# A hybrid decoder layer in fp32: pairs of tiles loaded as one, new homes for half of x, small transfers moved to GpSimd

## The chip, the cores and the metric

The kernel runs on one NeuronCore of a Trainium2 chip. The metric is the device time of one execution in microseconds (us); lower is better. The engines are PE (TensorE, matrix products, with its weight loads as PEld), DVE (VectorE), ACT (ScalarE), POOL (GpSimd) and SP (SyncE, which here only issues DMAs). Each takes its instructions strictly in the order in which they stand on its own queue. Data move between DRAM and the on-chip SBUF by DMAs, which two queues issue: SP's and GpSimd's.

## The reference

The layer takes x of 1024 tokens × 2048 channels and a memory of 256 tokens, all fp32:

```python
h = rmsnorm(x, ln_g)
proj = h @ w_in            # columns: g_u g_v g_z | d_q d_k d_v d_z d_a d_b | c_q c_z
out_a = gmlp_spatial_gating(g_u, g_v, gmlp_ws, gmlp_bs, gmlp_ln_g, gmlp_ln_b) * silu(g_z)
q, k, v = causal_conv_silu(concat(d_q, d_k, d_v), conv_w)      # 4 taps; q and k l2-normalised
g = -exp(dn_a_log) * softplus(d_a + dn_dt_bias); beta = sigmoid(d_b)
out_b = rmsnorm(gated_delta_rule(q, k, v, g, beta), dn_norm_g) * silu(d_z)   # 8 heads of 128
mk, mv = split(rmsnorm(mem, mem_norm_g) @ w_mem_kv)            # 4 heads of 128
out_c = softmax(c_q mk^T / sqrt(128)) mv * silu(c_z)
x = x + concat(out_a, out_b, out_c) @ w_out
return rmsnorm(x, final_g)
```

## The kernel before

**Precision.** An fp32 operand is split into a high part (`ahi`, `whi`: a cast to fp32r, which ACT does) and the rest (`alo`, `wlo`: a subtraction, on DVE), and each product is three matmuls: high·high, high·low, low·high.

**The big products.** The contraction over 2048 channels is cut into KT = 16 tiles of P = 128. The 1024 tokens are two halves of HT = 512. A product over a pair of column blocks is seen as a product of 2 × 2 block matrices (token half by contraction half, and contraction half by column block) and done with seven block products instead of eight, named m and run in the order 2, 1, 6, 5, 3, 7, 4. Their operands are blocks or sums and differences of blocks. `first_product` does it for the first six column tiles of the DeltaNet's q, k and v, straight from the prepared x in SBUF; `seven` does it for the five pairs of column blocks that follow (blocks 0 to 4), and for W_out. In `seven` the left operands come from DRAM for two contraction tiles at a time, by `h_left` (x's transposed blocks `h0_d`, `hT_d` and their sums `s_all`) or `m_left` (the gated mix and its sums `s_d`); the weights come in by `rights_made`, `rights_back` and, in the first product, `first_block` and `fetch`, and are combined by `meet`, `minus` and `add` on DVE. A block of weights of two contraction tiles is two DMAs of 256 KB, in the first product two or three for one tile.

**The stages.** To about 62 us the memory's K and V are made in 16 steps (`kvmark[k]` marks the end of step k), while `prep` makes the x rows 0 to 3 (a row is 128 tokens × 2048 channels in four tiles of 512): ACT squares the row and sums it up, POOL takes 1/rms (the 128x1 operations on `small`), DVE scales, PE transposes, and the result is split (`put0`). `kv_d` (kvd in the profile) takes the K and V, scaled, back to DRAM. To about 110 us comes `first_product(2)`, and beside it the second half of x, rows 4 to 7, is loaded, scaled and transposed (`prep1`; here ACT copies the transposed tile out of PE's banks `dn`), its sums are made (`left_sums`), and the per-token decays (`decay_rows`, `decay_mm`, `decays`). `first_product(1)` and the other five follow; from about 200 us the fronts (convolution, l2 norms, the q·k products in `qk`) run beside them, then blocks 0 to 4 with the DeltaNet's backs and the attention, W_out to about 1601 us, and the last normalisation.

**Buffers.** The small tiles have rings: `kT`, `qT`, `vs`, `kd` and `ai` of four tiles of 512 each, `ut`, `gt` and `inv` of two of 1024. Before the fronts need them they hold the rows of x: row 4 the halves of `ut`; row 5 two tiles of `kT` and two of `qT`; row 6 two of `kd` and two of `ai`; row 7 two of `vs` and the halves of a `gt`. Later the same tiles hold weight blocks (`kept`) and left operands (`araw`).

**The order.** The code records every operation in `Plan` before any is issued, which is why all instructions of the profile have line L300. `issue` then simulates the engines with a table of costs and gives every instruction its place: of what is ready on an engine, the one with the lowest `rank` first. `R.slow` and `R.land` are nanoseconds that it adds between another engine's result, or a landed load, and the PE instruction that uses it. They cost no time by themselves; a PE instruction with them takes a later place in PE's queue. `behind(op)` and `R.gate` keep an operation behind another.

Of the kernel before, what the change touches and what calls it, by code (L numbers as in the profile page):

```python
# [9 lines left out]
F32 = mybir.dt.float32  # L10
# [293 lines left out]
def kernel(  # L304
# [95 lines left out]
    et = [C([P, HT], f"et{i}") for i in range(2)]  # L400
    ring = {t: Slots(t, 4, [P, HT]) for t in ("kT", "qT", "vs", "kd", "ai")}
# [15 lines left out]
    h0_d = DT([KT, P, HT], "h0d")  # L417
    hT_d = DT([NH, P, HT], "hTd")
# [42 lines left out]

    def row_tiles(tag):
        if tag in ("inv", "gt", "ut"):
            return [b[:, i * HT : (i + 1) * HT] for b in (ring[tag](), ring[tag]()) for i in range(2)]
        return [ring[tag]() for _ in range(4)]
# [82 lines left out]
    def put0(tt):  # L548
        def put(q, tp):
# [9 lines left out]
            with rank(5):  # L559
                Q.dma_start(h0_d[4 * q : 4 * q + 4, :, tt * P : (tt + 1) * P].rearrange("k p n -> p k n"), t)  # L560
# [68 lines left out]
    for mt in range(2):  # L629
        t = [ring["ai"](F32R) for _ in range(2)]  # L630
# [3 lines left out]
        for i in range(2):  # L634
            with rank(2.5):
              Q.dma_start(
                kv_d[1, :, :, i, mt * P : (mt + 1) * P].rearrange("h p e -> p h e"),
                tok(t[i]).bitcast(F32),
            )
    with rank(2):  # L640
        prep(3, put0(3), spare, (2, 3, 0, 1))
    for h in range(NX):
        t = ring["vs"](F32R).rearrange("p (s m) -> p s m", s=2)
        with rank(2.2):
            split_to(t[:, 0], t[:, 1], kfs[h], V)
        with rank(2.5):
            Q.dma_start(kv_d[0, h], t.bitcast(F32))


    R.gate = kvmark[-1]  # L650
    G.affine_select(out=utri, in_=ones, compare_op=ALU.is_ge, fill=0.0, base=0,
                    pattern=[[1, P]], channel_multiplier=-1)
    with rank(3.5):
        Q.dma_start(rows[0:96], conv_w.rearrange("k (c p) -> (k c) p", p=P))
        Q.dma_start(rows[96:100], gmlp_ln_g[0].rearrange("(c p) -> c p", p=P))
        Q.dma_start(rows[100:104], gmlp_ln_b[0].rearrange("(c p) -> c p", p=P))
        Q.dma_start(rows[104:105], dn_norm_g)
    dtb = C([P, NH], "dtb")
    Q.dma_start(dtb, dn_dt_bias[0].partition_broadcast(P))
    nal = C([P, NH], "nal")  # L660
    Q.dma_start(nal, dn_a_log[0].partition_broadcast(P))
    S.activation(nal, nal, AF.Exp)
    V.tensor_scalar(nal, nal, -1.0, None, op0=ALU.mult)

    with rank(3.5):
# [3 lines left out]
        V.tensor_scalar(cw, pt[:, 0:96], 0.5, None, op0=ALU.mult)  # L669
        col2 = C([P, 9], "col2")  # L670
        V.tensor_copy(col2, pt[:, 96:105])

# [1239 lines left out]
```

## Time and profile before

| | |
|---|---|
| three runs | 1617.7, 1619.48, 1614.85 us; median 1617.7 |
| the profiled execution | 1613.38 us, its span 1611.4 us |
| granted TensorE clock, mean of the span | 0.996 of full speed |
| instructions | 26264 |
| DMA | 428.97 MB, mean 266 GB/s |
| HBM | read 337.49 MB, written 89.16 MB |

The span is the time from the first to the last instruction of the profiled execution. An engine's busy share is an average over stages, so the stretches are read one by one. In the rows of the trace, `out<-in` names the tile written and the tile read, "128x512" is partitions × elements, and the square bracket gives the time for which the engine stood idle before the instruction, and what released it.

### The profile page before, as it was taken

Reading aid. Unit: us, or ns where it says so; the run is one execution under the profiler, and the core shown is the slowest. Engines: PE = TensorE matmul, PEld = TensorE weight load, DVE = VectorE, ACT = ScalarE, POOL = GpSimd, SP = SyncE. Lnnn points to the kernel's source line nnn. Section 1 sums busy time; section 2 is a strip of 40 time slices with the busy share of each in tenths; the row PEclk is TensorE's granted clock in tenths of the full one; section 3 lists DMA queues with packets and bytes.
Section 4 is the critical chain, followed back from the end, with each engine's and each line's share of the span. In section 5 each row is a group of like instructions: output and inputs, shape, how many; then the busy total and the mean of one; then the engine's idle time right before and its main releaser. Section 6 shows DMA issues by size and latency. Waiting matters only on the chain.

```text
span 1611.4 us, 26264 instructions
## 1 busy us (share of the span) xinstructions
PE 1581.3 (98%) x8538; PEld 1325.7 (82%) x8538; DVE 1310.2 (81%) x2209; ACT 1023.9 (64%) x2185; POOL 310.8 (19%) x499
## 2 busy tenths in 40 slices
PE   9999999999999999999999999999999999999997
PEld 8878778778888888878888888888888888888886
DVE  6987797889899899887998777767778888789775
ACT  7843476576755688966676667767556774345355
POOL 0100023242311422335433333031000000000001
PEclk9999999999999999999999999999999999999999
DMA  9998878988679878888689775888867879588646
GB/s 358 299 273 238 263 221 257 327 306 273 223 252 317 271 241 279 311 308 272 213 265 362 249 235 168 273 305 285 300 224 261 260 248 351 191 279 290 215 146 240
DMA packets 264523, 428.97 MB, mean 266 GB/s; under 512 B 32905, under 2 KB 90306, under 8 KB 264386
## 3 DMA queue, kind: packets, MB, share of 16 engines
q1 hardware_dynamic: 241762, 371.03, 69.9%
q0 software_dynamic: 22016, 55.21, 10.2%
q8 instruction: 67, 1.10, 0.3%
q10 hardware_dynamic: 608, 1.06, 0.2%
q14 instruction: 70, 0.57, 0.1%
HBM read 337.49 MB, written 89.16 MB: 265 GB/s over the span
## 4 chain that ended last, share of the span: by engine, by line
PE 78%; DMA 9%; DVE 7%; ACT 2%; issue 2%; SPq 2%; POOL 0%; DVEq 0%; POOLq 0%; ACTq 0%
PE acc L300 55%; PE dn L300 23%; SPq L300 2%; DVE wlo L300 1%; DMA wraw<-in_w_in_dram 1%; DMA vs<-in_x_dram 1%; DVE qT L300 1%; DMA y<-in_w_in_dram 1%; DMA raws<-h0d 1%; DVE alo L300 1%; DMA qT<-in_w_in_dram 1%; DVE kT L300 1%; DMA kT<-in_w_in_dram 1%; DMA gd<-y2w 0%; ACT whi L300 0%
## 5 line engine op out<-in xcount | busy, mean ns | idle before, releaser
L300 PE MATMUL acc<-ahi,whi 128*128 128x512 f32 (+1 forms) x1328 | 455.5, 393 | 1.4 <-ACT y L300 1.4
L300 PE MATMUL acc<-ahi,wlo 128*128 128x512 f32 (+1 forms) x904 | 354.3, 393 | 0.0
L300 PEld LDWEIGHTS acc<-ahi,whi 128*128 128x128 f32 x1328 | 248.5, 188 | 50.3 <-ACT y L300 1.8
L300 PEld LDWEIGHTS acc<-ahi,wlo 128*128 128x128 f32 x904 | 169.9, 188 | 32.9
L300 ACT CAST ahi<-raws 128x1024 fp32r<-128x1024 f32 x141 | 147.8, 1048 | 62.5 <-PE dn L300 28.1
L300 PE MATMUL acc<-alo,whi 128*128 128x512 f32 (+1 forms) x480 | 187.5, 391 | 0.0
L300 PE MATMUL acc<-ahi,zh 128*128 128x512 f32 x424 | 167.7, 396 | 3.2 <-DVE y L300 3.2
L300 PE MATMUL acc<-ahi,zl 128*128 128x512 f32 x424 | 167.5, 395 | 0.0
L300 PE MATMUL acc<-alo,zh 128*128 128x512 f32 x424 | 167.0, 394 | 0.0
L300 POOL TENSOR_TENSOR small<-small,mhalf 128x1 f32<-128x1 f32 x26 | 20.4, 789 | 510.1 <-DVE small L300 510.1
L300 DVE TENSOR_TENSOR wlo<-wraw,whi 128x1024 fp32r<-128x1024 f32 (+1 forms) x80 | 94.3, 1179 | 22.1 <-ACT whi L300 19.9
L300 ACT CAST whi<-wraw 128x1024 fp32r<-128x1024 f32 (+1 forms) x80 | 81.4, 1017 | 47.9 <-PE acc L300 32.9
L300 PEld LDWEIGHTS acc<-alo,whi 128*128 128x128 f32 x480 | 90.7, 189 | 17.0
L300 DVE TENSOR_TENSOR alo<-raws,ahi 128x1024 fp32r<-128x1024 f32 x71 | 86.5, 1219 | 17.4 <-ACT ahi L300 17.1
L300 DVE TENSOR_TENSOR ahi<-raws,ahi 128x1024 fp32r<-128x1024 f32 x70 | 85.3, 1219 | 18.5 <-ACT ahi L300 18.2
L300 PEld LDWEIGHTS acc<-ahi,zh 128*128 128x128 f32 x424 | 79.9, 188 | 18.6 <-DVE y L300 3.6
L300 DVE TENSOR_TENSOR alo<-y,ahi 128x1024 fp32r<-128x1024 f32 x65 | 79.7, 1226 | 17.1 <-ACT ahi L300 16.9
L300 PEld LDWEIGHTS acc<-ahi,zl 128*128 128x128 f32 x424 | 79.9, 188 | 15.4
L300 PEld LDWEIGHTS acc<-alo,zh 128*128 128x128 f32 x424 | 79.9, 188 | 15.2
L300 ACT CAST ahi<-y 128x1024 fp32r<-128x1024 f32 x65 | 68.3, 1050 | 37.9 <-PE acc L300 19.5
L300 PE MATMUL dn<-whi,ahi 128*128 128x512 f32 x232 | 77.6, 389 | 0.0
L300 PE MATMUL acc<-whi,ahi 128*128 128x512 f32 x216 | 73.2, 392 | 0.0
(535 smaller groups left out, 3807.4 us busy)
## 6 DMA issues: line engine op xcount, KB each, us to landing
wraw<-in_w_in_dram SPq DMA_DIRECT2D x160, 256.0 KB, 4.3
raws<-sa SPq DMA_DIRECT2D x122, 256.0 KB, 4.2
y<-in_w_in_dram SPq DMA_DIRECT2D x80, 256.0 KB, 4.3
wraw<-in_w_out_dram SPq DMA_DIRECT2D x64, 256.0 KB, 4.3
raws<-h0d SPq DMA_DIRECT2D x58, 256.0 KB, 5.1
y<-sa SPq DMA_DIRECT2D x54, 256.0 KB, 4.3
raws<-sd SPq DMA_DIRECT2D x42, 256.0 KB, 3.0
y<-in_w_out_dram SPq DMA_DIRECT2D x33, 256.0 KB, 4.5
```

Of the source, the lines that this page charges most:

```text
L300: o.fn(*o.args, **o.kw)
```

## The change

The rings `kT`, `qT`, `vs`, `kd` and `ai` keep two tiles of 512, and the other two become one tile of 1024 each, the `twin` (`kTw` and so on). Weight blocks and left operands kept there are now one tile: one load, one cast, one subtraction of 1024 (768 in the first product) where there were two. `h0_d`, `hT_d` and `s_all` lie in DRAM by pairs of contraction tiles, so that a left pair is one load of 512 KB; `rows_of` and `twos_of` give the writes that shape, and a right operand taken from such a tile is read with a stride (`by_row`). `blk` covers two contraction tiles, `first_block` and `fetch` make a block one or two DMAs. The rows of x have other homes: row 4 the twins of `kd` and `vs`, row 5 the halves of `ut`, row 6 the halves of a `gt` and the twin of `ai`, row 7 the twins of `kT` and `qT`. The eight kvd stores and seven small loads go to GpSimd's queue; `R.slow` is 800 around the work on x's second half and around `qk`; the decay sums of the first half are made once after row 5, in another bank, and `decays` has rank 4.1 instead of 6.

In the built programs PE has the same number of matmuls of each form. SP has 1033 DMAs instead of 1518, GpSimd 391 instead of 376; DVE's additions and subtractions are 1291 instead of 1523, ACT's casts 573 instead of 643.

The places at which the order changes follow. On ACT, at the preparation of rows 4 to 7, before (`jk` takes the squares of an x tile, `small` their sum, `dn` is a bank with a transposed tile, `wraw` and `inv` hold weights):

```order
L300 ACTIVATE jk,small_97<-ai_390 128x512
L300 COPY xr_91<-dn_111 128x128
L300 ACTIVATE jk,small_98<-vs_391 128x512
L300 COPY kT_383<-dn_112 128x512
L300 COPY kT_384<-dn_111 128x512
L300 ACTIVATE jk,small_98<-vs_392 128x512
L300 ACTIVATE nal<-nal 128x8
L300 ACTIVATE jk,small_98<-gt_393 128x512
L300 COPY qT_385<-dn_112 128x512
```

and after:

```order
L300 ACTIVATE jk,small_102<-gt_376 128x512 x2
L300 ACTIVATE jk,small_102<-aiw 128x512 x2
L300 CAST inv_373<-wraw_71 128x768
L300 ACTIVATE jk,small_103<-kTw 128x512 x2
L300 CAST whi_73<-wraw_72 128x768
L300 ACTIVATE jk,small_103<-qTw 128x512 x2
L300 CAST whi_74<-inv_375 128x768
L300 COPY kdw<-dn_116 128x512
L300 COPY kdw<-dn_117 128x512
L300 COPY vsw<-dn_116 128x512
```

Before, the squares of row 7 (vs, gt) stand between the copies of row 5 (kT, qT); after, all squares of rows 6 and 7 stand ahead of the first copy of row 4 (kdw), with three weight casts among them. On SP the two loads of vs stood behind the third weight block of the first product; all x loads now stand ahead of it.

On SP, at the loads for the meets in `first_product(1)`, before (`in_w_in` is W_in; `pd` takes finished columns of the product; kd, kT and inv take pieces of weight blocks):

```order
L300 DMA pd_2_173<-y_394 128x512
L300 DMA kd_387<-in_w_in_dram 128x256
L300 DMA pd_0_179<-y_394 128x512
L300 DMA kd_388<-in_w_in_dram 128x256
L300 DMA kT_383<-in_w_in_dram 128x384
L300 DMA kT_383<-in_w_in_dram 128x128
L300 DMA pd_1_180<-y2w 128x512
L300 DMA inv_453<-in_w_in_dram 128x128 x2
L300 DMA inv_453<-in_w_in_dram 128x512
```

and after:

```order
L300 DMA pd_0_172<-y_377 128x512
L300 DMA kTw<-in_w_in_dram 128x512
L300 DMA kTw<-in_w_in_dram 128x2x128
L300 DMA pd_1_173<-y2w 128x512
L300 DMA inv_436<-in_w_in_dram 128x512
L300 DMA inv_436<-in_w_in_dram 128x2x128
L300 DMA pd_2_174<-y2w 128x512
L300 DMA raws<-sa_327 128x1024
L300 DMA aiw<-in_w_in_dram 128x512
L300 DMA aiw<-in_w_in_dram 128x2x128
```

A block is two DMAs where it was three or four, the stores of finished columns still stand between them, and a left pair (raws) is one load.

On POOL, at the end of the memory's product, before (`small_101` to `104` are the sums of four x rows; `utri` and `xr` are constants):

```order
L300 TENSOR_TENSOR small_101<-small_101,mhalf 128x1
L300 AFFINE_SELECT utri<-ones 128x128
L300 TENSOR_TENSOR small_102<-small_102,mhalf 128x1
L300 MEMSET xr_89 128x3
L300 MEMSET xr_90 128x3
L300 TENSOR_TENSOR small_103<-small_103,mhalf 128x1
L300 TENSOR_TENSOR small_104<-small_104,mhalf 128x1
```

and after (`small_108` is the sum of row 4):

```order
L300 TENSOR_TENSOR small_107<-small_107,mhalf 128x1
L300 DMA kvd<-ai_149 128x4x128
L300 DMA kvd<-ai_150 128x4x128
L300 DMA kvd<-kd_151 128x4x128
L300 DMA kvd<-kd_152 128x4x128
L300 AFFINE_SELECT utri<-ones 128x128
L300 DMA kvd<-vs_153 128x512
L300 DMA kvd<-vs_154 128x512
L300 MEMSET xr_94 128x3
L300 DMA kvd<-et_77 128x512
L300 DMA kvd<-et_78 128x512
L300 TENSOR_TENSOR small_108<-small_108,mhalf 128x1
```

The eight stores now stand between the 1/rms of row 3 and that of row 4. The seven small loads stand earlier on the same queue, ahead of the 1/rms of row 1.

The core of the diff:

```diff
-    ring = {t: Slots(t, 4, [P, HT]) for t in ("kT", "qT", "vs", "kd", "ai")}
+    et = [C([P, HT], f"et{i}", F32R) for i in range(2)]
+    for t in et:
+        R.users[t.tensor.name] = []
+    ring = {t: Slots(t, 2, [P, HT]) for t in ("kT", "qT", "vs", "kd", "ai")}
+    twin = {t: C([P, 2 * HT], f"{t}w") for t in ring}
...
-    h0_d = DT([KT, P, HT], "h0d")
-    hT_d = DT([NH, P, HT], "hTd")
+    h0_d = DT([KT // 2, P, 2 * HT], "h0d")
+    hT_d = DT([NH // 2, P, 2 * HT], "hTd")
...
-            return [b[:, i * HT : (i + 1) * HT] for b in (ring[tag](), ring[tag]()) for i in range(2)]
-        return [ring[tag]() for _ in range(4)]
+        return [ring[tag](), ring[tag](), *halves(twin[tag])]
+
+    def rows_of(d, q, tt):
+        return d[2 * q : 2 * q + 2, :, tt * 2 * P : (tt + 1) * 2 * P].rearrange("j p n -> p j n")
+
+    def twos_of(t):
+        return t.rearrange("p (j n) -> p j n", j=2)
...
-                Q.dma_start(h0_d[4 * q : 4 * q + 4, :, tt * P : (tt + 1) * P].rearrange("k p n -> p k n"), t)
+                Q.dma_start(rows_of(h0_d, q, tt), twos_of(t.rearrange("p k c -> p (k c)")))
...
-        t = [ring["ai"](F32R) for _ in range(2)]
+        t = [ring[("ai", "kd")[mt]](F32R) for _ in range(2)]
...
         for i in range(2):
             with rank(2.5):
-              Q.dma_start(
-                kv_d[1, :, :, i, mt * P : (mt + 1) * P].rearrange("h p e -> p h e"),
-                tok(t[i]).bitcast(F32),
-            )
+                G.dma_start(
+                    kv_d[1, :, :, i, mt * P : (mt + 1) * P].rearrange("h p e -> p h e"),
+                    tok(t[i]).bitcast(F32),
+                )
...
-        t = ring["vs"](F32R).rearrange("p (s m) -> p s m", s=2)
+        t = (ring["vs"](F32R) if h < 2 else et[h - 2]).rearrange("p (s m) -> p s m", s=2)
         with rank(2.2):
             split_to(t[:, 0], t[:, 1], kfs[h], V)
         with rank(2.5):
-            Q.dma_start(kv_d[0, h], t.bitcast(F32))
-
-
+            G.dma_start(kv_d[0, h], t.bitcast(F32))
...
+    R.gate = kvmark[8]
+    with rank(2.5):
+        for at, n, src in ((0, 96, conv_w.rearrange("k (c p) -> (k c) p", p=P)),
+                           (96, 4, gmlp_ln_g[0].rearrange("(c p) -> c p", p=P)),
+                           (100, 4, gmlp_ln_b[0].rearrange("(c p) -> c p", p=P)), (104, 1, dn_norm_g)):
+            G.dma_start(rows[at : at + n], src)
+        abf = ring["E"]()[:, 0 : KT * 16].rearrange("p (k c) -> p k c", c=16)
+        G.dma_start(abf, w_in[:, C_AB : C_AB + 16].rearrange("(k p) c -> p k c", p=P))
+        dtb = C([P, NH], "dtb")
+        G.dma_start(dtb, dn_dt_bias[0].partition_broadcast(P))
+        nal = C([P, NH], "nal")
+        G.dma_start(nal, dn_a_log[0].partition_broadcast(P))
...
-    s_all = [DT([NH, P, HT], f"sa{i}") for i in range(4)]
-    s_d = [[[t[j] for t in s_all] for j in range(NH)],
-           [[DT([P, HT], f"sd1_{j}_{i}") for i in range(4)] for j in range(NH)]]
+    s_all = [DT([NH // 2, P, 2 * HT], f"sa{i}") for i in range(4)]
+    s_d = [[DT([P, HT], f"sd1_{j}_{i}") for i in range(4)] for j in range(NH)]
...
     def blk(w, k, c0):
-        return w[k * P : (k + 1) * P, c0 : c0 + HT]
-
-    def whole(k):
+        return w[k * P : (k + 2) * P, c0 : c0 + HT].rearrange("(u p) c -> p u c", u=2)
...
+            V.tensor_tensor(out=tok(t), in0=ahq[q][:, tt], in1=alq[q][:, tt], op=ALU.add)
+            Q.dma_start(rows_of(h0_d, q, tt), twos_of(t))
...
-        mm(a, wk, ahi[k], k == NH, False)
-        mm(a, wk, alo[k], False, k == NH - 1)
+        mm(a, wk, ahi[k], k == 0, False)
+        mm(a, wk, alo[k], False, k == KT - 1)
...
             hs = ring["hs"]()
+            R.slow = 800.0
             kd, ai, _ = qk(h, hf, q, k, hs, gt)
+            R.slow = 0.0
...
-        return [w_in[k, c0 : c0 + n] for c0, n in FIRST_COLS[b]]
+        qk = w_in[k, C_Q : C_Q + 2 * DW].rearrange("p (s c) -> p s c", s=2)
+        return [qk[:, :, 0 : 3 * P]] if b == 0 else [w_in[k, C_DV : C_DV + HT], qk[:, :, 3 * P : 4 * P]]
+
+    def by_row(a, u):
+        return [x_.rearrange("p (t u c) -> p u t c", u=2, c=P)[:, u] for x_ in a]
...
-        for d, x_ in pieces(dst, blk_):
-            Q.dma_start(d, x_)
+
+        if len(blk_) == 2:
+            v, qk = cuts(dst)
+            Q.dma_start(v, blk_[0])
+            Q.dma_start(twos_of(qk), blk_[1])
+        elif len(dst) == 1:
+            Q.dma_start(twos_of(dst[0]), blk_[0])
+        else:
+            a, b = dst
+            Q.dma_start(a[:, 0 : 3 * P], blk_[0][:, 0])
+            Q.dma_start(a[:, 3 * P :], blk_[0][:, 1, 0:P])
+            Q.dma_start(b, blk_[0][:, 1, P:])
...
-            return [x_[:, u * HT : (u + 1) * HT] for x_ in lefts]
+            return by_row(lefts, u)
...
-    two = [[ring[tag](slot=k) for k in (2, 3)] for tag in ("kT", "qT", "kd", "ai", "vs")]
-    tiles = [[t[:, j * HT : (j + 1) * HT] for t in ring["ut"].bufs for j in range(2)],
-             two[0] + two[1], two[2] + two[3], two[4] + halves(ring["gt"]())]
-    for tag in ("kT", "qT", "vs", "kd", "ai"):
-        ring[tag].turn = (0, 1)
+    tiles = [halves(twin["kd"]) + halves(twin["vs"]), [h for t in ring["ut"].bufs for h in halves(t)],
+             halves(ring["gt"]()) + halves(twin["ai"]), halves(twin["kT"]) + halves(twin["qT"])]
...
+    R.slow = 800.0
     with rank(4):
         for i in range(NT):
             prep1(i)
             decay_rows(strips, i)
+            if i == 1:
+                a = work()
+                for k in range(KT):
+                    decay_mm(a, k)
+                S.copy(sums0, a[0:32])
...
-    for k in (*range(NH, KT), *range(NH)):
-        decay_mm(dnr.bufs[2], k)
-    with rank(6):
+    for q in range(NQ // 2, NQ):
+        for tt in range(H0, NT):
+            whole(q, tt)
+    with rank(4.1):
         decays(1, strips, lambda: dnr.bufs[3])
-        decays(0, dnr.bufs[2], lambda: dnr.bufs[2])
+        decays(0, sums0, lambda: dnr.bufs[2])
+    R.slow = 0.0
...
-    kept, vs01 = two[:4], two[4]
-    more = halves(heir(alq[2], "y3", "alo2"))
+    kept, vs01 = [[twin[t]] for t in ("kT", "qT", "kd", "ai")], halves(twin["vs"])
...
-    araw = over([kept[3], vs01, *([t] for t in raws)])
+    araw = over([[twin["vs"]], [twin["qT"]], *([t] for t in raws)])
...
-        for i, x_ in enumerate(src):
-            t = ts[i] if len(ts) == 2 else ts[0][:, i * HT : (i + 1) * HT]
-            Q.dma_start(t, x_)
+        if len(ts) == 1 and not isinstance(src, list):
+            Q.dma_start(twos_of(ts[0]) if src.ndim == 3 else ts[0], src)
+            return ts
+        for i in range(2):
+            t = ts[i] if len(ts) == 2 else halves(ts[0])[i]
+            Q.dma_start(t, src[i] if isinstance(src, list) else src[:, i])
...
-            return loaded([s_d[0][j][SUM[m]] for j in js])
-        return loaded([hT_d[j] if m == 4 else h0_d[j + NH * (m == 2)] for j in js])
+            return loaded(s_all[SUM[m]][n])
+        return loaded(hT_d[n] if m == 4 else h0_d[n + NH // 2 * (m == 2)])
...
-                    load2(ts, [blocks(0, 1, j) for j in js])
-            r = plain([blocks(*((1, 1) if m in (7, 5) else AT[m]), j) for j in js])
-            parts = [(t, r[:, i * HT : (i + 1) * HT]) for i, t in enumerate(ts)]
+                    load2(ts, blocks(0, 1, js))
+            r = plain(blocks(*((1, 1) if m in (7, 5) else AT[m]), js))
+            parts = [(ts[0], r)]
```

132 lines of the change are left out of this document (52 added, 80 removed).

## The prediction

> **What bounds the kernel.** I read the page first, then the stretches, what PE waits for, and the chain of waits.
>
> ```profile
> PE 1581.3 (98%) x8538; PEld 1325.7 (82%) x8538; DVE 1310.2 (81%) x2209; ACT 1023.9 (64%) x2185; POOL 310.8 (19%) x499
> ```
>
> PE is busy for 1581.3 us of a span of 1611.4. The built programs hold the same matmuls in both kernels, 7744 of the same forms, so the work of the bound doesn't change, and all there is to win is PE's 30 us of idle time and the time in which it ran at a lowered clock. The stretches say where those lie (columns: from:to, length, busy of PE, PEld, DVE, ACT, POOL with counts, granted clock, DMA share, GB/s):
>
> ```profile
> 0.00:60.00 60.00, 58.17 (x380) 52.36 (x381) 43.41 (x66) 47.14 (x91) 6.05 (x14) 1.00 0.96 334
> 60.00:90.00 30.00, 25.66 (x208) 22.25 (x207) 26.95 (x57) 20.57 (x49) 4.25 (x6) 1.00 0.93 278
> 90.00:100.00 10.00, 7.52 (x62) 6.29 (x63) 5.86 (x12) 6.25 (x16) 0.86 (x1) 0.83 0.92 296
> 165.00:175.00 10.00, 7.30 (x18) 5.07 (x19) 6.90 (x12) 0.00 (x0) 0.00 (x0) 0.66 0.95 304
> 200.00:210.00 10.00, 7.80 (x39) 6.34 (x38) 9.86 (x18) 9.97 (x28) 0.76 (x3) 1.00 0.73 208
> 350.00:600.00 250.00, 250.00 (x1161) 208.53 (x1160) 228.54 (x377) 167.13 (x340) 77.95 (x124) 1.00 0.81 267
> 600.00:1000.00 400.00, 395.71 (x2511) 333.90 (x2510) 330.07 (x586) 287.11 (x665) 138.35 (x225) 1.00 0.80 267
> 1600.00:1611.40 11.40, 2.70 (x12) 1.89 (x11) 3.62 (x9) 3.56 (x8) 1.10 (x2) 0.82 0.82 304
> ```
>
> From 350 to 600 PE has no idle time at all, though DVE is 91% busy there and the DMA engines 81%. The idle time is early, with 4.3 us between 600 and 1000 and the tail, which the change leaves alone. DMA is near its limit only at the start (0.96). PE's own waits, with total, count and longest:
>
> ```profile
> PE dn L300 <- ACT kT L300: 3.6, 1, 3.6
> PE dn L300 <- DVE kT L300: 3.5, 2, 2.2
> PE acc L300 <- DVE y L300: 3.2, 1, 3.2
> PE dn L300 <- DVE ai L300: 2.0, 3, 1.2
> ```
>
> **The change, part by part.** (a) Homes and loads of x's second half. The longest wait is behind row 7's loads:
>
> ```profile
> 86.18 0.98 SPq L300 DMA_DIRECT2D vs<-in_x_dram  x2
> 91.23 0.63 ACT L300 ACTIVATE jk<-vs 128x512 bf16<-128x512 f32 x1 [4.25 <-DMA vs<-in_x_dram]
> 91.86 1.05 ACT L300 COPY kT<-dn 128x512 f32<-128x512 f32 x2
> 92.48 1.97 PE L300 MATMUL dn<-ident,qT 128*128 128x128 f32 x8 [3.62 <-ACT kT L300]
> ```
>
> SP issues the vs loads at 86.18. ACT, which takes its queue in order, stands 4.25 us for them, ahead of the copies that free PE's banks, and PE stands 3.62. The clock then is 0.83 for 10 us, worth 10 × 0.17 = 1.7. In the new order all x loads of the second half stand in SP's queue ahead of the third weight block, and ACT's squares of all four rows ahead of the first copy of row 4. A late load would now be met at the squares, where PE has memory products and sums of the first half to run. I take the whole of it: 3.62 + 1.7 = −5.3. What is late next is ACT's casts of the weights that stand between those squares.
>
> (b) Weight pieces at the meets of first_product(1).
>
> ```profile
> 118.45 4.21 SPq L300 DMA_DIRECT2D y<-in_w_in_dram  x8
> 160.56 5.50 DMA kT<-in_w_in_dram
> 166.19 0.69 DVE L300 TENSOR_TENSOR y<-kT,y 128x512 f32<-128x512 f32 x1 [3.15 <-DMA kT<-in_w_in_dram]
> 167.54 0.79 PE L300 MATMUL acc<-ahi,zh 128*128 128x512 f32 x1 [3.18 <-DVE y L300]
> ```
>
> A block that is issued at 160.56 lands 5.50 us later; DVE waits 3.15 at the head of its queue with evacuations behind it, PE 3.18, and at clock 0.66 for 10 us another 3.4: 6.6 in all. An issue costs SP 4.21/8 = 0.53. The change makes two issues of three or four for a block and drops others: SP's DMAs fall from 1518 to 1033 in the built programs. SP comes to the block earlier, but the meets still stand between evacuations on DVE, so that a late block would stop PE as before. Ends −6.6 and 0; half, −3.3, since no row decides.
>
> (c) The 800 ns that the planner puts between another engine's result and PE, for x rows 4 to 7 and for q and k. It is no instruction; it only moves PE's consumers later in order.
>
> ```profile
> 204.98 0.68 DVE L300 SCALAR_TENSOR_TENSOR kT<-tn,kT 128x512 f32<-128x512 f32 x1
> 205.72 0.66 PE L300 MATMUL dn<-ident,kT 128*128 128x128 f32 x4 [2.19 <-DVE kT L300]
> ```
>
> PE waits for kT twice and for ai three times. 0.8 of each at the most gives 2 × 0.8 + 2.0 = 3.6 (the three ai waits are 2.0 together). Ends −3.6 and 0 (DVE and ACT are full at 200:210, 9.86 and 9.97 of 10, so the producers may be late by more); half, −1.8.
>
> (d) x row 2 or 3 now has two loads, of 0.5 MB together, ahead of a memory weight block at the start. At 334 GB/s those are 0.5/0.334 = 1.57 us. ACT's cast there started without a wait:
>
> ```profile
> 18.34 1.16 ACT L300 ACTIVATE whi<-wraw,gcol 128x1024 fp32r<-128x1024 f32 x1
> 18.05 0.55 POOL L300 TENSOR_TENSOR small<-small,mhalf 128x1 f32<-128x1 f32 x1 [16.53 <-DVE small L300]
> 64.41 1.19 POOL L300 TENSOR_TENSOR small<-small,mhalf 128x1 f32<-128x1 f32 x1 [13.65 <-DVE small L300]
> 73.98 1.29 SPq L300 DMA_DIRECT2D kvd<-vs  x2
> 76.67 0.60 PE L300 MATMUL dn<-ident,ut 128*128 128x128 f32 x4
> 205.96 0.57 POOL L300 DMA_DIRECT2D late<-kT  x1 [3.77 <-DVE kT L300]
> ```
>
> Ends 0 and +1.6; half, +0.8.
>
> (e) GpSimd takes seven small loads and eight kvd stores from SP, and they stand ahead of the x rows' 1/rms on its queue (the same rows as above). The loads cost 7 × 0.57 = 4.0 ahead of row 1, whose 1/rms POOL did long before PE asked: 0. The stores hold row 4: the last kvd data were there at 75.3 (73.98 + 1.29), then the issue, 0.57, the 1/rms, up to 1.19, and a DVE scale like the 0.68 of (c): 77.7. PE transposed row 4 from 76.67; in the new order about 5 us more of matmuls stand ahead of it. The margin is 4 us: 0, with ends 0 and +7.2 (margin gone: 3.8 and, as in (b), 3.4 of clock).
>
> (f) Two loads of 256 KB as one of 512 KB, from block 0 to W_out; half the left operands and all the weights. They matter where a landing decides. The chain of waits has nine such links between 598 and 705, and this is the first, the last, and what they came to:
>
> ```profile
> 598.39 6.49 DMA wraw<-in_w_in_dram
> 699.95 4.12 DMA raws<-h0d
> 704.00 0.72 PE L300 MATMUL acc<-ahi,whi 128*128 128x512 f32 x2 [1.38 <-ACT y L300]
> ```
>
> A merged load lands later than the first of two, perhaps earlier than the second. The DMA rows (KB each, us to landing):
>
> ```profile
> ut<-in_w_mem_kv_dram SPq DMA_DIRECT2D x8, 512.0 KB, 7.1
> wraw<-in_w_in_dram SPq DMA_DIRECT2D x160, 256.0 KB, 4.3
> gt<-gtd POOLq DMA_DIRECT2D x8, 512.0 KB, 5.1
> kT<-late POOLq DMA_DIRECT2D x16, 256.0 KB, 4.7
> ```
>
> In one queue, POOL's, 512 KB took 0.4 more than 256, and an issue of 0.53 is saved: about 0. On SP the 512 KB rows took 7.1 against 4.3, though at the start, with the DMA engines at 0.96: 7.1 − 4.3 − 0.5 = +2.3 a link, nine links +21. At the other end PE's idle time there goes: 1.38, and a second one of 1.2 in the same stretch, −2.6. I take 0, since 600:1000 has 0.80 of DMA and so is nearer the POOL rows than the start.
>
> The Trainium skill, "DMA: Bandwidth & Descriptors", section "Anatomy of one DMA — SWDGE (gpsimd) path", fits one DMA as 2.0 us and its bytes at 436 GB/s, so 256 KB more are 0.6 us by an estimate from it. By that, (f) would be 9 × (0.6 − 0.53) = +0.6 and the sum 1609; the 7.1 and 4.3 here disagree with it at the start, the POOL rows nearly agree.
>
> (g) DVE and ACT do less, in wider instructions:
>
> ```profile
> L300 DVE TENSOR_TENSOR alo<-raws,ahi 128x1024 fp32r<-128x1024 f32 x7 | 8.5, 1217 | 1.0 <-ACT ahi L300 1.0
> L300 DVE TENSOR_TENSOR alo<-ai,ahi 128x512 fp32r<-128x512 f32 x10 | 6.8, 686 | 3.0 <-ACT ahi L300 3.0
> L300 DVE TENSOR_TENSOR wlo<-inv,whi 128x768 fp32r<-128x768 f32 x6 | 5.7, 951 | 0.9 <-ACT whi L300 0.9
> L300 DVE TENSOR_TENSOR wlo<-kd,whi 128x256 fp32r<-128x256 f32 x6 | 2.5, 416 | 0.0
> ```
>
> In the built programs 398 of 512 wide and 62 of 256 go, 174 of 1024 and 54 of 768 come: 398 × 0.686 + 62 × 0.416 − 174 × 1.217 − 54 × 0.951 = 35 us off DVE. What hides it is PE, never idle at 350:600 under a DVE as busy as that; where DVE is full, at 200:210, the instructions are the fronts', which the change leaves alone. 0, ends −2.2 (PE's idle time there) and 0. Right operands read with a stride, decay sums in another bank and at an earlier rank: the same matmuls; 0.
>
> The sum is −5.3 − 3.3 − 1.8 + 0.8 = −9.6. The profiled execution took 1613.38, so 1603.8; the three runs have their median 4.3 above it (1617.7), which I add: 1608.
>
> **Rivals.** *More of it.* (b), (c) and (f) in full and (d) at 0: −5.3 − 6.6 − 3.6 − 2.6 = −18.1, so 1600. For it: fewer issues help every late load at once. Against: nothing in the stretches says that SP is what is late after 350.
>
> *The waits come back.* ACT's squares stop for a late x load with weight casts behind them, and the meets stop for their blocks as before: (a) and (b) at 0 leave −1.0, 1617; one of the two, 1611 to 1613. For it: the DMA engines are at 0.92 to 0.96 whenever PE waits early, and the bytes don't change. Against: in (a) the load is issued behind weights that are used later.
>
> *Slower: merged loads land late.* At +2.3 a link (f) is +21, and 1608 + 21 = 1629. It turns the sign where a link is later by over 9.6/9 = 1.1 us. For it: the 7.1 row. Against: 350:600 without idle time says most loads have slack.
>
> *POOL's stores hold row 4.* Eight issues and the 1/rms between DVE's instructions: POOL's small operation took 0.55 when DVE was quiet and 1.19 at 64.41. If each issue were stretched by 1.0 the stores take 8 us more, the margin of (e) is gone: +5.5 to +7.2, 1613.5 to 1615. Against: the DMA issue at 205.96 took 0.57 with DVE at 9.86 of 10. The Trainium skill, "SBUF — State Buffer", section "SBUF: two separate sides", has a rule for this: a DMA from GpSimd's queue cannot write its descriptors while DVE runs an operation that locks the port they share, and goes from 620 ns to 3100; it would have these stores on SP. The 0.57 here doesn't agree.
>
> **How the numbers follow.** The forecast has 0.43, 1608, with 1603 to 1613 as its own range from the ends of (b) to (d); more of it 0.17; waits back 0.22; merged loads late 0.13; POOL's stores 0.05. A measurement of this kernel can tell about 0.3% from no change: 1612.9 to 1622.5. Faster: 0.17, nearly all of 0.43 and little of the waits: 0.60. Within: most of the waits, POOL and a rest: 0.26. Slower: the late merged loads and 0.01: 0.14. From 1596 to 1620 the range leaves out the merged loads and the end of more of it.
>
> **What would show it.** (a) No PE wait on an ACT copy of rows 4 to 7, and clock 1.00 around 95. (b) Clock 1.00 around 170 and no DVE wait for a weight block with PE behind it. (c) The waits for kT and ai in the fronts shorter by 0.8 each. (d) ACT's casts from 18 to 30 without a DMA wait. (e) Row 4's 1/rms done before PE's transposes. (f) 600:1000 with no more than 4.3 us idle, and 512 KB rows near 5. (g) DVE's busy time near 1275, PE's at 1581. Wrong it would be if 512 KB rows read 7 on SP after 350, or if a new wait of over 3 us stands before 110.

## The result, and the profile after

The changed kernel takes 1595.74 us (median of four, 1595.46 to 1596.26); the kernel before, on the same chip, 1616.61 (four, 1614.85 to 1619.48). The ratio is 0.987, with an interval of 0.9852 to 0.9887: 20.9 us faster, where 9.7 were forecast, and 0.3 us below the low end of the range. The profiled execution took 1595.59 us with a span of 1593.8, so the two profiles differ by 17.8.

The page's first line, then the stretches and PE's waits, as they stand in the prediction for before:

```profile
PE 1572.7 (99%) x8538; PEld 1322.8 (83%) x8538; DVE 1293.5 (81%) x1977; ACT 1015.7 (64%) x2113; POOL 311.5 (20%) x514
```

```profile
0.00:60.00 60.00, 55.52 (x365) 49.60 (x365) 42.31 (x65) 46.93 (x89) 8.17 (x20) 1.00 0.97 344
90.00:100.00 10.00, 10.00 (x101) 7.92 (x103) 8.10 (x14) 4.08 (x7) 1.11 (x2) 1.00 0.57 159
165.00:175.00 10.00, 10.00 (x46) 8.29 (x45) 9.97 (x18) 7.00 (x10) 0.00 (x0) 1.00 1.05 385
200.00:210.00 10.00, 10.00 (x46) 8.29 (x45) 9.89 (x13) 9.83 (x26) 4.89 (x5) 1.00 0.65 209
210.00:300.00 90.00, 87.60 (x417) 73.12 (x417) 72.68 (x117) 54.19 (x120) 24.26 (x37) 1.00 0.86 279
350.00:600.00 250.00, 250.00 (x1170) 208.94 (x1169) 227.16 (x340) 169.22 (x347) 75.08 (x126) 1.00 0.79 260
600.00:1000.00 400.00, 398.56 (x2538) 337.95 (x2537) 330.50 (x548) 289.02 (x671) 142.01 (x238) 1.00 0.81 274
```

```profile
PE dn L300 <- DMA E<-in_gmlp_ws_dram: 2.4, 1, 2.4
PE acc L300 <- ACT whi L300: 2.3, 3, 1.6
PE dn L300 <- DVE ai L300: 0.3, 1, 0.3
```

The stretches at 90, 165 and 200 us have neither idle time nor a lowered clock any more. PE's idle time fell from 30.1 to 21.1 us. Its busy time fell by 8.6 us with the same count; the lowered clock at 90 and 165 us before accounts for 5.1 of them (1.7 and 3.4). Two waits are new: at 20 us for ACT's whi (1.6), and 2.4 for a load of gmlp_ws. DVE is still as full at 200:210 and at 350:600.

To see where the time went I counted PE's instructions in order, each with the median time of its shape from its start to the next one's, the smaller of the two traces' medians (0.227 us for 128x512), and compared when this sum, PE's work, reached the same value:

| PE's work, us | in the trace before, us | gained (−) or lost | the prediction's term |
|---|---|---|---|
| 0 to 20 | 1 to 25 | +1.9 | (d), +0.8 |
| 60 to 80 | 68 to 97 | −6.1 | (a), −5.3 |
| 140 to 160 | 162 to 189 | −6.7 | (b), −3.3 |
| 160 to 180 and 260 to 340 | 189 to 211, 292 to 375 | −2.3 and −3.5 | (c), −1.8 |
| 240 to 260 | 272 to 292 | +2.6 | none |
| 660 to 680 | 697 to 720 | −3.2 | (f), 0 |
| the rest | | −2.1 | 0 |
| behind the last matmul | 1602.7 to 1611.4 | +1.9 | (e), 0 |

The last row is no instruction of an engine's work. The last issue is the same in both traces, at 1606.40 and 1586.87 us, and the span ends 5.0 and 6.9 us later (ACT, too, issues a few DMAs, four of them stores of the output; a_sp_small below tells where the 1.9 us come from):

```profile
1586.87 0.34 ACTq L300 DMA_DIRECT2D out_dram<-y2w  x1
```

The DMA rows answer (f): the merged loads of 512 KB take 5.1 us where those of 256 KB took 4.3, near POOL's rows and far from the 7.1 at the start.

```profile
wraw<-in_w_in_dram SPq DMA_DIRECT2D x80, 512.0 KB, 5.1
ut<-in_w_mem_kv_dram SPq DMA_DIRECT2D x8, 512.0 KB, 7.7
```

### The profile page after: what moved, and what is told of

It reads as the page before. It is cut to its first block, busy times and chain, and to the rows that moved or that the text cites. A ratio compares the mean times of both kernels' runs of the same rounds, so it can differ in the third digit from the quotient of the medians.

```text
span 1593.8 us, 25244 instructions
## 1 busy us (share of the span) xinstructions
PE 1572.7 (99%) x8538; PEld 1322.8 (83%) x8538; DVE 1293.5 (81%) x1977; ACT 1015.7 (64%) x2113; POOL 311.5 (20%) x514
## 4 chain that ended last, share of the span: by engine, by line
PE 89%; DMA 5%; DVE 2%; issue 1%; ACT 1%; POOL 0%; SPq 0%; POOLq 0%; DVEq 0%; ACTq 0%
PE acc L300 63%; PE dn L300 26%; DMA ut<-in_w_mem_kv_dram 1%; DMA E<-in_gmlp_ws_dram 1%; DVE wlo L300 1%; DMA vsw<-in_x_dram 1%; DMA inv<-in_w_in_dram 0%; DMA kd<-in_x_dram 0%; DMA vsw<-gd 0%; DVE alo L300 0%; POOL inv L300 0%; DMA aiw<-in_x_dram 0%; SPq L300 0%; DMA gdr<-gt 0%; DMA tblk<-tdrearly 0%
## 5 line engine op out<-in xcount | busy, mean ns | idle before, releaser
L300 ACT CAST whi<-wraw 128x1024 fp32r<-128x1024 f32 (+1 forms) x78 | 80.5, 1033 | 62.4 <-PE acc L300 41.4
```

The lines of the kernel that those rows point to most:

```text
L300: o.fn(*o.args, **o.kw)
```

## The experiments

**Loads and operations split again, in the order of after.** These three keep every engine's order, and cut only the instruction as it is issued.

`e_fetch_pieces`, the weight blocks of the first product in the pieces of before (the second edit does the same for the third block's halves):

```diff
-            Q.dma_start(twos_of(dst[0]), blk_[0])
+            # one place in the order, three issues
+            (d[:, 0:384], blk[:, 0]), (d[:, 384:512], blk[:, 1, 0:128]), (d[:, 512:], blk[:, 1, 128:])
```

> The kernel after, with the order of every engine unchanged, but the weight blocks of the first product issued on SP in as many pieces as before (3 for 384+384 columns, 3 for the third block); 92 more issues. Theory A (the wait at 164 us before was SP's issuing: it issued without a pause from 114 to 164): the wait for a weight block before the meets comes back, PE stands 3 us or more between 120 and 175 us, clock below 1.00 there, 1595.7 + 3 to 6.6 = 1599 to 1602. Rival B (DVE's and ACT's wider operations and the new order removed it): within 1 us of 1595.7.

Measured: 1603.77 us (1601.07 to 1610.21), ratio to before 0.9926 (0.9902 to 0.9949). Theory A by the time, but not at the place that it named: from 120 to 175 us PE stands only 0.5 us, at a clock of 1.00, and the wait of 3.2 for y did not come back. SP's share of time spent issuing from 120 to 165 us, summed from its rows, was 0.83 before, 0.56 after and 0.64 here. The profile is of the slowest execution, 14.6 us over after's; between 140 and 280 us of PE's work it loses 7.8, and 3.7 are the start's, which differs between executions (below). The blocks are late again: DVE's waits for blocks of W_in from 120 to 270 us come to 16.1 us before, 2.8 after and 24.6 here (9.1 of them in one wait that ends at 122 us). PE's waits between 100 and 300 us here, of which after has the first alone (2.4):

```profile
PE dn L306 <- DMA E<-in_gmlp_ws_dram: 3.2, 1, 3.2
PE acc L306 <- DVE wlo L306: 1.8, 2, 1.3
PE dn L306 <- DVE sc L306: 1.1, 1, 1.1
```

The first of them is no measure of SP. The load of gmlp_ws is issued 8.1 us later than in after, but PE comes to it 7.8 us later too; what PE waits for is the landing, 9.7 us behind the issue here and 9.3 in after.

`e_fetch_two` tells issues from short pieces:

```diff
-            Q.dma_start(twos_of(dst[0]), blk_[0])
+            # one place in the order, two issues of 384 columns
+            (halves(dst[0])[i], blk_[0][:, i]) for i in range(2)
```

> The kernel after, same order on every engine; each two-column load of a weight block of the first product is issued as two DMAs along the cut that it has anyway (384 and 384 columns, or 128 and 128), so that the rows moved stay the same pieces of DRAM and only SP's issues grow. Theory A (the 8 us of the finer pieces were SP's issuing, which made later loads late): 1598 to 1602. Rival B (they were the short pieces of 512 bytes): within 1 us of 1595.7.

Measured: 1599.19 us (1595.64 to 1603.09): theory A by the median, though one of the four runs is at after's time. DVE's waits for blocks of W_in from 120 to 270 us come to 15.5 us (3.1 in e_dve_two, which has after's issues), and the trace, of the slowest run, shows how one reaches PE:

```profile
163.53 0.96 DVE L306 TENSOR_TENSOR wraw<-kTw,wraw 128x768 f32<-128x768 f32 x1 [1.47 <-DMA kTw<-in_w_in_dram]
167.93 0.50 PE L306 MATMUL acc<-ahi,wlo 128*128 128x512 f32 x1 [1.60 <-DVE wlo L306]
```

Its 62 more issues cost 3.5 us, the 92 and the shorter pieces 8.0. SP's issuing is a part of it, shown; how the rest divides between issues and pieces is not.

`e_load2_two`:

```diff
-            Q.dma_start(twos_of(ts[0]) if src.ndim == 3 else ts[0], src)
+            # one place in the order, two issues
+            (halves(ts[0])[i], the i-th half of src) for i in range(2)
```

> The kernel after, same order on every engine, but each merged load of 512 KB of the blocks 0 to 4 and of W_out issued as two of 256 KB; 360 more issues. Theory A (the merged loads brought the 3 us between 660 and 680 us of PE's work because SP gets to the late links sooner): PE's idle time between 600 and 720 comes back by 2 to 4 us, 1598 to 1600. Rival B (the order and the other homes brought them): within 1 us of 1595.7. Rival C (a 512 KB load lands later than the second of two): faster than 1595 by up to 2 us.

Measured: 1596.09 us (1594.85 to 1602.27). Rival B: no worth of the merged loads of the blocks and of W_out can be seen, and nothing comes back between 660 and 680 of PE's work. `a_split_load2`, the same cut in `load2`, known to the planner:

> The kernel after with each merged load of 512 KB of the blocks and of W_out as two of 256 KB, this time known to the planner, which makes a new order with 360 more issues on SP. Theory A (merging these loads is worth nothing, in the order either): within 2 us of 1595.7. Rival B (its worth is the order that the planner can make with fewer issues): 1599 or more, with waits between 600 and 900 us as before.

Measured: 1597.84 us (1595.16 to 1599.77): 2.1 us over after, at the edge of theory A's 2 and below rival B's 1599. Its profile has no new wait of over 0.7 us behind 600; 1.7 of what it loses are at the wait for gmlp_ws.

`e_dve_two`:

```diff
-                o.fn(*o.args, **o.kw)
+                for sl in (slice(0, 512), slice(512, w)):   # DVE, 768 or 1024 wide, on a twin
+                    o.fn(out=k["out"][:, sl], in0=k["in0"][:, sl], in1=k["in1"][:, sl], op=k["op"])
```

> The kernel after, same order on every engine, but every addition or subtraction of 1024 or 768 columns on a twin done on DVE in two instructions (222 more, some 24 us more of DVE). Theory A (DVE's saved time counts for nothing, as PE never waits where it is hidden): within 1 us of 1595.7. Rival B (it is what took the waits at 164 us and in the fronts away): DVE is late there again, PE waits for y, kT or ai come back, 1598 to 1602.

Measured: 1595.66 us (1595.41 to 1595.96). Theory A by the time. But the zero may hold two terms: DVE is busy 14.2 us more, PE waits three times for ai, 1.9 us in all (0.3 in after, 1.1 in after's second trace), and 2.8 us are lost between 580 and 660 of PE's work, while the wait of 2.4 for gmlp_ws is absent, as the load landed 6.6 us behind its issue here. No edit touched that load. So (g) is small, and not shown to be exactly zero.

**The 800 ns.** `a_noslow_fronts`, in a new order:

```diff
-            R.slow = 800.0
             kd, ai, _ = qk(h, hf, q, k, hs, gt)
-            R.slow = 0.0
```

> The kernel after without the 800 ns around qk in the fronts; the planner orders everything behind the first front anew. Theory A (the 800 ns took PE's waits for kT and ai in the fronts away, 5.5 us in all before): 3 to 5.5 us slower, 1599 to 1601, with PE waits for DVE kT and DVE ai. Rival B (DVE being less full took them away): within 1 us of 1595.7.

Measured: 1603.04 us (1597.70 to 1604.49). The profile is of the 1597.70, with one wait for ai of 3.0 us near 690. The same kernel again:

> The kernel after without the 800 ns around qk, a second trace of it, since the first was of its fastest run. Theory A (the waits for kT and ai in the fronts are what the 800 ns take away): waits of 3 to 6 us in all between 195 and 330 us. Rival B (they do nothing there; the order that is planned without them meets the stretch at 830 to 860 us, where the DMA engines are full, at a bad place): no such waits, and a loss of 4 to 8 us behind 700 us.

Measured: 1601.44 us (1600.23 to 1603.09). Its waits are not at 200 to 340, where PE has no idle time in this kernel, but at 690, in a later front:

```profile
689.55 0.58 PE L300 MATMUL dn<-inv 128*128 128x256 f32 x1 [3.90 <-DVE ai L300]
```

The stretches of this kernel, then of after, at the same place:

```profile
680.00:690.00 10.00, 6.09 (x27) 4.78 (x27) 10.00 (x13) 8.09 (x21) 0.67 (x2) 0.88 0.69 229
690.00:700.00 10.00, 10.00 (x41) 8.25 (x40) 7.27 (x13) 3.77 (x6) 7.59 (x8) 0.78 0.70 228
```

```profile
680.00:690.00 10.00, 10.00 (x50) 8.42 (x48) 9.00 (x14) 9.48 (x23) 2.84 (x5) 1.00 0.99 338
690.00:700.00 10.00, 10.00 (x49) 8.37 (x48) 9.50 (x15) 7.61 (x21) 2.86 (x5) 1.00 0.81 263
```

DVE is busy for all of 680:690, PE stands 3.9 us for the product of the front's qk that DVE has not yet evacuated, and the clock is 0.88 and 0.78: between 660 and 680 of PE's work this costs 6.5 us. Theory A's mechanism stands, at another place than it named; rival B's place, 830 to 860, shows nothing. In the trace before the same wait stands at 708:

```profile
708.47 0.39 PE L300 MATMUL dn<-inv 128*128 128x256 f32 x1 [1.22 <-DVE ai L300]
```

`a_noslow_x` leaves out the other 800 ns, around `prep1` and `decays`:

> The kernel after without the 800 ns around the preparation of x's second half and the decays (those around qk stay). Theory A (the rows' copies are on time without them): within 1 us of 1595.7. Rival B (PE stands for DVE's scales or ACT's copies of rows 4 to 7): 2 to 5 us slower, with waits between 75 and 125 us.

Measured: 1597.39 us (1595.79 to 1599.91); its profiled run took 1595.88, without a new wait between 75 and 125 us. Nothing that can be told apart. `a_noslow_both` leaves out both:

> The kernel after without any of the new 800 ns. Theory A: the sum of the two edits alone, 7.3 + 1.7, 1604 to 1606. Rival B (each order has its own luck): anything from 1596 to 1610 that is not that sum.

Measured: 1601.54 us (1599.93 to 1602.02), as without those in the fronts alone and not the sum: rival B. `b_slow`, the kernel before with both:

```diff
+            R.slow = 800.0
             kd, ai, _ = qk(h, hf, q, k, hs, gt)
+            R.slow = 0.0
...
+    R.slow = 800.0                 # to behind decays
     with rank(4):
         for i in range(NT):
             prep1(i)
```

> The kernel before with the 800 ns around x's second half and around qk, and nothing else. Theory A (the 800 ns by themselves take away the fronts' waits for kT and ai): 4 to 7 us off, 1609 to 1612, with the waits at 92 and 164 us still there. Rival B (they only do so where SP and DVE have room, as in the kernel after): within 2 us of 1616.4, the waits moved to other places.

Measured: 1618.11 us (1611.80 to 1619.70), ratio 1.0017 (1.0004 to 1.003). To 680 of PE's work its profile is 8.7 us ahead of before's, 3.1 of them at 660 to 680, as in after; PE's waits for kT in the fronts fall from 3.5 to 1.0. From 740 to 840 it loses 13.4, of which 5.2 are near 782 us (a wait of 2.1 for DVE) and 9.5 here:

```profile
850.00:860.00 10.00, 6.97 (x34) 5.49 (x32) 7.66 (x14) 5.61 (x9) 2.06 (x5) 0.92 1.10 379
860.00:870.00 10.00, 7.32 (x60) 6.05 (x58) 7.01 (x15) 5.46 (x16) 1.16 (x2) 0.57 1.07 392
```

The DMA engines are full there (1.10), PE stands twice, and the clock is 0.57. Before and after pass this stretch, as full, without idle time. So the 800 ns alone are worth nothing to before; what its profile wins to 680, the new order gives back.

**The homes.** `b_homes`:

```diff
-        t = [ring["ai"](F32R) for _ in range(2)]
+        t = [ring[("ai", "kd")[mt]](F32R) for _ in range(2)]
...
-        t = ring["vs"](F32R).rearrange("p (s m) -> p s m", s=2)
+        t = (ring["vs"](F32R) if h < 2 else et[h - 2]).rearrange("p (s m) -> p s m", s=2)
```

> The kernel before with one edit: the K and V on their way to kvd take other tiles (ai, kd, two of vs and et, as in the kernel after), so that the homes of x rows 6 and 7 are free while these are loaded. Theory A (PE's 3.62 us wait for ACT's copy of kT was row 7's loads waiting for tiles that still held K and V): that wait is gone, clock 1.00 at 90 to 100 us, 4 to 6 us off PE's work between 60 and 80: 1616.4 - 5.3 = 1611. Rival B (SP reached the loads late for its many issues, whatever the tiles): the wait stays, within 2 us of 1616.4.

Measured: 1612.62 us (1608.69 to 1617.60), ratio 0.9986 (0.9974 to 0.9999): 2.3 us below before on the same chip (1614.89), where theory A had 5.3. The profile is of the slowest of its ten runs. SP's row for row 7's loads, at 86.18 before:

```profile
39.88 0.50 SPq L300 DMA_DIRECT2D vs<-in_x_dram  x1
90.00:100.00 10.00, 10.00 (x113) 8.16 (x113) 8.90 (x19) 6.01 (x15) 2.39 (x2) 1.00 1.01 291
```

Theory A's mechanism: the loads go out as soon as the tiles are free, the wait at 92 us is gone, and 4.3 us are won at 60 to 80. Some come back: 4.1 at the start (row 6's loads now go ahead of the memory's weights, as in after), and PE still waits in the fronts, which cost 3.6 and 3.8 us more than before:

```profile
PE dn L300 <- DVE kT L300: 5.8, 2, 3.5
```

`a_sp_small`, in which `G.dma_start` is `Q.dma_start` again for the kvd stores and the small loads:

> The kernel after with the eight kvd stores and the seven small loads back on SP. Theory A (they cost nothing on either queue): within 1 us of 1595.7. Rival B (on SP they delay the loads of x's second half by 15 issues, some 7 us, as SP was what was late before): 2 to 5 us slower between 60 and 110 us. Rival C (on GpSimd they held row 4's 1/rms): faster than 1594.7.

Measured: 1596.30 us (1595.45 to 1598.87). Theory A by the time, but its profile holds two terms that go against each other. On SP the seven small loads stand from 40.04 us on, and an x row's load behind them goes out at 46.99 us, where it went at 41.41 in after:

```profile
41.41 0.60 SPq L300 DMA_DIRECT2D kTw<-in_x_dram  x1
```

```profile
46.99 0.36 SPq L300 DMA_DIRECT2D kTw<-in_x_dram  x1
51.77 0.63 ACT L300 ACTIVATE jk<-kTw 128x512 bf16<-128x512 f32 x1 [4.31 <-DMA kTw<-in_x_dram]
1589.63 0.34 ACTq L300 DMA_DIRECT2D out_dram<-y2w  x1
```

ACT waits 4.3 us for it, PE 3.1 for ACT at 53 us, and 4.5 are lost from 47 to 74 us: rival B's mechanism, at an earlier row. The last row is the last issue; the span of 1594.8 us ends 5.1 behind it. In all fifteen traces with 391 DMAs on GpSimd the end comes 6.8 to 6.9 us behind the last issue, in the four with 376 (before, b_homes, b_slow and this one) 5.0 to 5.1. So the fifteen transfers on GpSimd cost 1.8 us at the very end; by what mechanism is not shown. The wait of 2.4 at 267 is also gone here, which alone would be worth 2.6.

**The two new waits.** `v1`:

```diff
+            with behind(kvmark[9] if i == 2 else R.gate):
...
+        R.land = 6000.0
         Q.dma_start(wt, gmlp_ws[0].rearrange("g t s -> t g s"))
+        R.land = 0.0
```

> The kernel after with two edits: the loads of x row 6 start only after step 9 of the memory's product, and the planner counts 6 us more between the load of gmlp_ws and PE's transposes of it. Theory A (the two new waits, 1.6 us at 20 us and 2.4 us at 267 us, are these loads): both gone, 1591 to 1593. Rival B (what is gained comes back in the newly planned order): 1594 to 1597.

Measured: 1606.13 us (1603.16 to 1608.21). Both waits are gone, and the profile is 3.5 us ahead of after's at 760 of PE's work. But the order behind them is new, and loses 13.1 from there to 840, at b_slow's place:

```profile
840.00:850.00 10.00, 5.76 (x52) 4.59 (x50) 6.52 (x13) 5.37 (x14) 2.13 (x4) 0.67 1.10 391
850.00:860.00 10.00, 9.09 (x82) 8.56 (x83) 7.90 (x16) 6.25 (x22) 2.66 (x6) 0.50 0.86 304
```

`v1_land`, the second edit alone:

> The kernel after with only the 6 us for gmlp_ws. Theory A: the wait at 267 us gone, that at 20 us as it was, 1593 to 1594. Rival B: the order behind it is new and takes 1 to 4 us back.

Measured: 1606.84 us (1603.06 to 1608.08): rival B, and more than it said, at the same place. `w_both` keeps after's order, and adds to the planned time of these instructions alone before the sort:

```diff
+        for o in self.ops:
+            o.at += o.shift            # 25000 for the two loads of row 6, 4000 for token_mix behind its loads
         self.ops.sort(key=lambda o: (o.at, o.idx))
```

> The kernel after with its order kept, but for two moves: the two loads of x row 6 that stood ahead of the memory's weights stand 17 rows later on SP, and the transposes and products on gmlp_ws stand 4 us later on PE and DVE. Theory A (the waits at 20 and 267 us are these, and the new orders of v1 lost their 10 us at 830 to 860 us by themselves): both waits gone, 1591 to 1593, no loss behind 800 us. Rival B (something else is late at 20 and 267 us): 1595 to 1597.

In it the token mixing adds its bias after the tile of that bias has been refilled, so the values differ, not the work. Measured: 1595.27 us (1593.70 to 1595.72), beside it after once more, `after_again`:

> The kernel after once more, for a second trace and for times on the same chip as w_both. Theory: 1595.5 to 1596.3 as before, the waits at 20 and 267 us at the same places. Rival (the tight times were chance): a spread of over 3 us, as the kernel before has.

Measured: 1595.79 us (1593.97 to 1597.12): the same median and a spread of 3.2 us, so the first four were closer together than the kernel is. In w_both both waits are gone and only 1.0 us is lost behind 800, but 1.6 us at the first mem tiles and 1.2 at 50 us are new. `w_aiw` moves the two loads alone:

> The kernel after with its order kept, except that the two loads of x row 6 ahead of the memory's weights stand 17 rows later on SP. Theory A: ACT's wait of 2 to 2.6 us for the weights of step 4 and PE's of 1.3 to 1.6 at 20 us are gone, 1593 to 1595. Rival B (the first loads' landing differs by as much from one execution to the next): 1595 to 1596, with the wait gone and another of its size within the first 10 us.

Measured: 1594.67 us (1594.43 to 1599.80). ACT's row for the weights of step 4, of after and of w_aiw:

```profile
20.89 1.15 ACT L300 ACTIVATE whi<-wraw,gcol 128x1024 fp32r<-128x1024 f32 x1 [2.60 <-DMA wraw<-in_w_mem_kv_dram]
```

```profile
19.20 1.14 ACT L304 ACTIVATE whi<-wraw,gcol 128x1024 fp32r<-128x1024 f32 x1
50.95 0.66 PE L304 MATMUL dn<-ident,kdw 128*128 128x128 f32 x4 [1.52 <-ACT tn L304]
```

The loads are the wait at 20 us: between 16 and 27 us 1.9 us come back. Without it another of 1.5 us stands at 51, and the first 10 us ran at a clock of 0.88. The wait at 267 us is gone here too, though nothing was moved for it: the load of gmlp_ws landed 6.6 us behind its issue, as in e_dve_two, where it took 9.3 in after and 8.9 in after_again. So w_both does not show that the later place removed that wait. The 1.1 us to after can't be told from nothing; it is not shown that any version here beats after.

## Why the prediction was wrong

The sign was right, and PE is still the bound; the size was not. The sum's −9.6 stands against −17.8 between the profiles. Two steps failed most: (b), put in at half where the whole wait went, and the 4.3 us that were added behind the sum.

- **(a)**, taken as −5.3, reads −6.1. b_homes shows the cause of the wait: the tiles, which held K and V, not SP's queue as such.
- **(b)**, the largest miss. The wait at 164 us was put in at half of 6.6, "since no row decides". It went in full, −6.7. A row did decide: SP's issues stood in rows almost without a pause from 114 us on, the block was late because SP was, and the change took 18 of SP's 77 issues from 120 to 165 us away. e_fetch_pieces and e_fetch_two give some of them back, DVE waits for its blocks again, and they lose 8.0 and 3.5 us. Not all of the 6.7 need be SP's: b_homes and b_slow, whose SP issues for 0.83 and 0.84 of that time, lose 2.2 and 2.4 us less here than before, as their waits for y and y2w come to 2.6 and 1.8 us and the clock stays at 1.00. That the meets "still stand between evacuations" was true and did not matter, since the blocks were no longer late.
- **(c)**, taken as −1.8: PE's waits in the fronts from 195 to 360 us, 3.5 for kT and 1.3 for ACT, went, −5.8 in all, past the end of −3.6. But without the 800 ns they stay away too, so that the step was right for a reason that the runs don't bear out. What removed them is not shown: none of e_fetch_pieces, e_load2_two and e_dve_two brings them back, b_homes keeps them, and in b_slow the 800 ns shorten them; the order of after as a whole is what is left, untried alone. The 800 ns around qk are worth 5.7 to 7.3 us by the medians of the two measurements, most of it at a later front.
- **(d)**, taken as +0.8, reads +1.9, just over its end of +1.6. w_aiw shows that it is the loads.
- **(e)**: row 4's 1/rms was in time, as said; after has no wait of PE of over 0.9 us between 60 and 110. But the term was not 0. Taking the small loads off SP spared a wait that cost 4.5 us in a_sp_small, and the end grew by 1.9, though the prediction said of the tail that the change leaves it alone. The Trainium skill's "SBUF — State Buffer", section "SBUF: two separate sides", has a GpSimd store stall while DVE runs an operation in a mode that takes the port they share, an fp32 copy within SBUF for one. After's rows on POOL, and the stretch around them:

```profile
67.38 1.55 POOL L300 DMA_DIRECT2D kvd<-ai  x2
74.67 0.54 POOL L300 DMA_DIRECT2D kvd<-et  x1 [1.19 <-ACT jk L300]
70.00:80.00 10.00, 8.61 (x72) 8.16 (x71) 9.46 (x25) 9.38 (x25) 5.61 (x9) 1.00 1.03 395
```

An issue took 0.54 to 0.78 us with DVE busy for 9.46 of 10. DVE's rows beside these issues hold no such copy, so the rule was neither seen at work nor refuted.
- **(g)**: 35 us off DVE were worked out, 16.7 measured (1310.2 to 1293.5), and e_dve_two puts 14.2 back. The 0 holds within some 3 us.
- **(f)** is 0 as a price of merging (e_load2_two), and the rival of late merged loads fell: 5.1 us, not 7. By the Trainium skill's "DMA: Bandwidth & Descriptors", section "Anatomy of one DMA — SWDGE (gpsimd) path", they would land 0.6 us later than 256 KB, an estimate from its fit for GpSimd's path; 0.8 was measured, on SP's queue, which is near it. But at 660 to 680 3.2 us were won: the second wait there, counted under (f) as 1.2, was a front's wait for ai (708.47), so it belonged to (c), where it was counted too. It is the 800 ns that take this wait away: b_slow wins 3.1 there, and a_noslow_fronts_2 loses 6.5.
- **Not in the sum**: the load of gmlp_ws, +2.6. Its tile came free at 259 us, and it landed 9.3 us after its issue. With a landing of 6.6 to 7.0 us, as in e_load2_two, e_dve_two and w_aiw with the load at the same place, PE does not wait; so this is a narrow margin of the order, and what it costs differs between executions.
- **The 4.3 us** from the profile to the median were carried over to the changed kernel as a constant. After's median lies 0.15 over its profile. Before's runs spread over 1610.9 to 1621.5 us in all comparisons, and the profiled one was among the quick ones. This step made 4 us of the 12 that the forecast was off.

Without the constant the rival "more of it" gives 1613.4 − 18.1 = 1595.3. Its chance was put at 0.17 because "nothing in the stretches says that SP is what is late after 350": the gain did not need that, most of it lay before 350. That its sum comes so near is luck in part: it has (d) at 0, no wait for gmlp_ws and no longer end, and 2.6 for (f).

## What to carry to other kernels

Read the issuing queue like an engine: where its rows stand almost without a pause and a consumer waits for what it issues last, issues taken away can bring the whole wait, and elsewhere (360 of the 485 issues removed here) no gain was seen. A stall can cost the clock besides its idle time: waits of 3.2, 3.6 and 3.9 us came to 6.6, 5.3 and 7.3 here. It need not: behind 3.1 us at 274 us of e_fetch_two and 3.0 at 686 of a_noslow_fronts the clock stayed at 1.00. So the clock is added only where the stretch shows it lowered. An experiment whose time says "nothing" can hold two terms that cancel (a_sp_small, e_dve_two): its trace is read as well. An edit to a planned order must be priced with the new order behind it: here that took back 13 us at one full stretch, so small edits are better made by moving the instructions than by planning anew.

## What was not expected of the hardware

Waits of nearly the same length cost very different clocks: 3.7 us of PE's waiting at 844 us of v1, with 1.4 more at 851, gave 0.67 and 0.50 in two stretches of 10 us, while 3.62 at 92 us before gave 0.83 in one, and 3.1 in e_fetch_two nothing. The start is not repeatable: PE's wait for the first memory weight (for DVE's whi) was 1.1, 0.9 and 1.8 us in after, after_again and w_both, whose first 10 us hold the same instructions, and the clock of these 10 us was 1.00, 1.00 and 0.89; together that is about what moving the two loads of row 6 is worth. And fifteen transfers moved to GpSimd's queue, none of them near the end, made the end 1.8 us longer.
